# A constant tile made 288 bytes wider, in a hybrid decoder block on one core

## The chip, the cores and the metric

The kernel runs on one core of a Trainium2 chip. The metric is the device time of one launch in microseconds (us), the median over several runs. A profile is one execution of the program, recorded by the hardware profiler; its times are counted from the first instruction.

## What is computed

A sequence of 2048 rows of 1024 numbers, with 16 learned rows ahead of it, goes through one decoder layer in float32. Cut to what matters here:

```python
n1 = rmsnorm(h, norm1_g)
proj = n1 @ w_in                                  # 1024 -> 512 (S5 group) + 512 (pooling group)
ys = s5_mixer(proj[..., :512], ...)               # complex diagonal scan, GELU, GLU
yp = pool_mixer(proj[..., 512:], ...)             # trailing means over 2/4/8/16, linear map
h = h + concat([rmsnorm(ys), rmsnorm(yp)]) @ w_out
n2 = rmsnorm(h, norm2_g)
ff = silu(n2 @ w_gate) * (n2 @ w_up)              # 1024 -> 2816, twice
h = h + ff @ w_down                               # 2816 -> 1024
out = rmsnorm(h, final_norm_g)
```

The three large products of the last part (gate, up, down) are most of the arithmetic.

## The kernel before

**Products in three parts.** Every float32 operand of a large product is split into a high part (rounded to the type that TensorE multiplies, `fp32r`) and a low part (the rest). `split` writes the high part with ScalarE (L110) and the low part with VectorE (L85). `mm3` then makes three matmuls for one product of a 128x128 block with a 128x512 block:

```python
def mm3(o, lh, ll, rh, rl, first, last):          # L116
    PE.matmul(o, lh, rh, start=first, stop=False) # L117
    PE.matmul(o, lh, rl, start=False, stop=False) # L118
    PE.matmul(o, ll, rh, start=False, stop=last)  # L119
```

The second argument is the stationary operand (128x128, loaded into the array by a weight load ahead of the matmul), the third the moving operand (128x512, read through while the matmul runs). In the profile a matmul is written out<-moving,stationary: `pr<-xt3h,wch` reads `xt3h` as the moving operand.

**Stages.** (1) 0 to 300 us: input projection, parameters of the S5 group, scans; its large matmuls are `pj`, with the weights `wh`, `wl` moving. (2) 300 to 577 us: gates and output projection, large matmuls `po`, again with `wh`, `wl` moving. (3) 577 to 1450 us: the gate and up products, `pr`. (4) 1450 to 1884 us: the down product, `pd`, final norm and output.

**Stage 3.** `gate_up` runs for two halves of the sequence (`b`) and 11 pairs of column blocks (`f0`), and calls `seven` twice, for gate and for up: 44 calls. `seven` is one step of Strassen's scheme in its seven-product form: instead of eight products of 512-wide blocks it makes seven, each of 4 blocks x 3 matmuls = 12 matmuls, with additions before and after. The seven moving operands are tiles called `xb11`, `xb21`, `xt2`, `xt3`, `xt1`, `xt4`, `xb22`, in this order of use, each as a high and a low tile of 128 x 4 x 512 float32. The stationary operands `wch`, `wcl` are split from the loaded weights `raw` (and from their sums `s`) just ahead of use, into ten buffers each.

**Stage 4.** The same scheme over the down product: 7 products x 8 row blocks = 56 accumulations of 11 blocks x 3 matmuls. The moving operand is the split down weight, held in chunks of four blocks in four slots (`db11`, `db21`, `dt2`, `dt3`) that take turns; these slots are the stage 3 tiles of the same names without the d. The stationary operands `fh`, `fl` come from `fr`, loaded from memory.

**Where the tiles lie.** SBUF is handed out as two stacks in each partition: pools opened on the left grow upwards from the low addresses, pools opened with `side="right"` grow downwards from the top. The order of the pools' opening and the sizes of the tiles fix every address. In the program before these are, in bytes from the partition's start:

| side | tiles | begin at | modulo 512 |
|---|---|---|---|
| left | `ident`, `ones`, `mhalf` | 16512, 17024, 17056 | 128, 128, 160 |
| left | `xb11`, `xb21`, `xb22`, `xt1` (high and low; `db11`, `db21` in stage 4) | 22208 to 79552, 8192 apart | 192 |
| left | `raw`, `hr`, `xp`, `wr`, `dwr` (four shared buffers) | 87744 to 100032; end at 104128 | 192 |
| right | `xt2`, `xt3`, `xt4` (high and low; `dt2`, `dt3` in stage 4) | 104416 to 145376, 8192 apart | 480 |
| right | `wch`, `wcl` (`fh`, `fl`) | 188384 to 227296, 2048 apart | 480 |
| right | `wh`, `wl` (moving in stages 1 and 2) | 163808 to 221152 | 480 |
| right | `xh`, `xl`, `mh`, `ml` (stationary in stages 1 and 2) | 104672 to 133344 | 224 |

In stages 3 and 4, 288 bytes are free between the end of the left stack and the beginning of the right one.

**The touched tile.** `mhalf` holds the exponent -0.5. It is filled once (L127) and read by GpSimd's power instruction in `rsqrt_into` as `mhalf[:n, :m]`, with `m` of 1, 2 or 8. It is the third tile of the first left pool, so that all other large left tiles lie above it.

**What sets the order.** The kernel is written in the order of the loops; the build puts the instructions of each engine in order by its own estimate of times, and adds the semaphore waits. Nearly all transfers are issued from SyncE's queue.

Of the kernel before, what the change touches and what calls it, by code (L numbers as in the profile page):

```python
# [9 lines left out]
F32 = mybir.dt.float32  # L10
# [6 lines left out]
P = 128  # L17
# [7 lines left out]
T = 8  # L25
# [12 lines left out]
def kernel(  # L38
# [30 lines left out]
    const = ctx.enter_context(tc.tile_pool(name="const", bufs=1))  # L69
# [53 lines left out]
    make_identity(nc, ident)  # L123
    ones = const.tile([P, 1], F32, name="ones")
    V.memset(ones, 1.0)
    mhalf = const.tile([P, 2 * T], F32, name="mhalf")
    V.memset(mhalf, -0.5)  # L127
    ss2 = const.tile([P, 2, NB * T], F32, name="ss2")
    rs2 = const.tile([P, NB * T], F32, name="rs2")
# [1125 lines left out]
```

## Time and profile before

| what | value |
|---|---|
| runs | 1882.72, 1887.77, 1888.33 us; median 1887.77 |
| the profiled execution | 1885.98 us, span of its instructions 1884.2 us |
| granted TensorE clock, mean | 0.988 |
| TensorE matmuls | busy 97% of the span, 8497 instructions |
| VectorE, ScalarE, GpSimd | busy 65%, 36%, 43% |
| transfers | 298.37 MB, mean 158 GB/s |

A matmul's row names its line, its operands and its duration. Matmuls are pipelined: one of 0.39 us starts some 0.23 us after the one before. So the time that a stream of them takes is read from the starts in the timeline, not from the durations.

### The profile page before, as it was taken

What the parts mean: (1) busy time and instruction counts of PE and PEld (TensorE: products, weight loads), DVE (VectorE), ACT (ScalarE), POOL (GpSimd) and SP (SyncE); (2) the same over time, 40 slices, a digit from 0 to 9 for tenths busy, and PEclk for the clock granted to TensorE, in tenths of its full rate; (3) what the DMA queues carried; (4) which work ended last, traced back from release to release, by engine and by line L of the source; (5) the groups of instructions that cost most, each with busy time, mean ns of one, the idle gap of its engine ahead of it and who ended that gap; (6) DMA issues with size and microseconds to landing.
All of it is one profiled execution on the core that took longest, in us unless ns stands there. A gap on an engine that the chain in (4) does not pass through costs nothing.

```text
span 1884.2 us, 23676 instructions
## 1 busy us (share of the span) xinstructions
PE 1822.9 (97%) x8497; PEld 1495.4 (79%) x8497; DVE 1232.4 (65%) x1913; ACT 673.8 (36%) x1213; POOL 816.9 (43%) x619
## 2 busy tenths in 40 slices
PE   7989997899999999999999999999999999999998
PEld 5767786788887888888887788888888888888886
DVE  6996777866457866656667866766666444445763
ACT  4333334243454333332334332333223343333441
POOL 1684425633344565453656866665662000003400
PEclk9999998999999999999999999999999999999999
DMA  6255424444355344443436554554447765536771
GB/s 182 72 176 183 144 96 145 174 168 140 112 175 167 106 157 140 140 157 107 156 117 211 194 166 151 163 179 150 133 150 228 227 198 170 154 109 208 245 218 69
DMA packets 260518, 298.37 MB, mean 158 GB/s; under 512 B 17148, under 2 KB 204048, under 8 KB 255536
## 3 DMA queue, kind: packets, MB, share of 16 engines
q1 hardware_dynamic: 260304, 296.84, 49.5%
q8 instruction: 67, 1.10, 0.2%
q14 instruction: 51, 0.42, 0.1%
q0 software_dynamic: 96, 0.01, 0.0%
HBM read 202.37 MB, written 96.53 MB: 159 GB/s over the span
## 4 chain that ended last, share of the span: by engine, by line
PE 73%; DVE 3%; DMA 2%; POOL 1%; issue 1%; ACT 1%; DVEq 0%; POOLq 0%; ACTq 0%
PE pr L117 14%; PE pr L118 14%; PE pr L119 14%; PE pd L117 8%; PE pd L118 8%; PE pd L119 8%; PE po L117 2%; PE po L119 2%; PE po L118 2%; DVE wcl L85 1%; PE pgate L774 1%; DMA hr<-h_d 1%; PE ptx L865 1%; DMA xp<-xr_d 0%; PE ppool L760 0%
## 5 line engine op out<-in xcount | busy, mean ns | idle before, releaser
L110 ACT CAST wch<-raw 128x512 fp32r<-128x512 f32 x176 | 108.7, 621 | 268.2 <-PE pr L118 240.8
L85 DVE TENSOR_TENSOR wcl<-raw,wch 128x512 fp32r<-128x512 f32 x176 | 175.7, 1001 | 37.4 <-ACT wch L110 37.0
L85 DVE TENSOR_TENSOR fl<-fr,fh 128x512 fp32r<-128x512 f32 x168 | 116.9, 707 | 126.3 <-ACT fh L110 126.2
L110 ACT CAST fh<-fr 128x512 fp32r<-128x512 f32 x168 | 96.2, 584 | 202.4 <-PE pd L118 175.0
L110 ACT CAST wch<-s 128x512 fp32r<-128x512 f32 x132 | 82.1, 622 | 224.2 <-PE pr L118 174.6
L85 POOL TENSOR_TENSOR s<-raw 128x512 f32<-128x512 f32 x44 | 67.8, 1540 | 174.7 <-DVE wcl L85 75.3
L85 DVE TENSOR_TENSOR wcl<-s,wch 128x512 fp32r<-128x512 f32 x132 | 118.3, 896 | 19.4 <-ACT wch L110 19.1
L85 POOL TENSOR_TENSOR db22h<-db22h,hd 128x512 f32<-128x512 f32 x4 | 5.2, 1292 | 256.2 <-DVE db22h L85 256.2
L117 PE MATMUL pj<-wh,xh 128*128 128x512 f32 x256 | 102.6, 409 | 2.6 <-ACT xh L110 2.3
L117 PE MATMUL po<-wh,mh 128*128 128x512 f32 x256 | 103.8, 406 | 0.7 <-ACT mh L110 0.7
L119 PE MATMUL pj<-wh,xl 128*128 128x512 f32 x256 | 103.0, 407 | 0.0
L118 PE MATMUL pj<-wl,xh 128*128 128x512 f32 x256 | 102.7, 403 | 0.0
L119 PE MATMUL po<-wh,ml 128*128 128x512 f32 x256 | 100.4, 393 | 0.8 <-DVE ml L85 0.8
L118 PE MATMUL po<-wl,mh 128*128 128x512 f32 x256 | 100.7, 393 | 0.0
L85 POOL TENSOR_TENSOR rs<-rv,mhalf 128x1 f32<-128x1 f32 (+2 forms) x35 | 31.5, 900 | 154.1 <-DVE rv L91 144.8
L85 POOL TENSOR_TENSOR wr<-wr 128x512 f32<-128x512 f32 x44 | 66.8, 1519 | 72.4 <-DMA wr<-in_w_down_dram 64.5
L85 DVE TENSOR_TENSOR gt<-gt,ut 128x512 f32<-128x512 f32 x88 | 92.9, 1057 | 0.0
L85 POOL TENSOR_TENSOR tmp<-z,pk 64x512 f32<-64x512 f32 x32 | 50.8, 1588 | 79.8 <-issue 64.7
L85 DVE TENSOR_TENSOR gt<-pr,gt 128x512 f32<-128x512 f32 x66 | 45.5, 690 | 60.3 <-PE pr L119 60.1
L85 POOL TENSOR_TENSOR ut<-gt 128x512 f32<-128x512 f32 x22 | 33.6, 1528 | 107.2 <-DVE gt L85 107.2
L117 PE MATMUL pr<-xt2h,wch 128*128 128x512 f32 x176 | 70.5, 400 | 5.3 <-DVE gt L85 3.6
L1006 ACT ACTIVATE gt<-gt 128x512 f32<-128x512 f32 x88 | 55.6, 633 | 50.8 <-DVE gt L85 50.8
(392 smaller groups left out, 5586.1 us busy)
## 6 DMA issues: line engine op xcount, KB each, us to landing
fr<-ff_d SPq DMA_DIRECT2D x56, 704.0 KB, 4.9
raw<-in_w_gate_dram SPq DMA_DIRECT2D x44, 512.0 KB, 4.8
raw<-in_w_up_dram SPq DMA_DIRECT2D x44, 512.0 KB, 4.3
ff_d<-gt SPq DMA_DIRECT2D x22, 1024.0 KB, 3.9
pk<-pk_d SPq DMA_DIRECT2D x16, 1284.0 KB, 6.2
ff_d<-ut SPq DMA_DIRECT2D x22, 768.0 KB, 5.6
wr<-in_w_down_dram SPq DMA_DIRECT2D x22, 512.0 KB, 3.3
wd_d<-wr SPq DMA_DIRECT2D x22, 512.0 KB, 3.4
```

Of the source, the lines that this page charges most:

```text
L85: e.tensor_tensor(o, a, b, op=op)
L110: A.copy(hi, src)
L117: PE.matmul(o, lh, rh, start=first, stop=False)
L118: PE.matmul(o, lh, rl, start=False, stop=False)
L119: PE.matmul(o, ll, rh, start=False, stop=last)
L774: PE.matmul(pg[:, k * P:(k + 1) * P], glubd[:, k], gt[:, k], start=True, stop=True)
L865: PE.transpose(pt[:, k], r[:, (4 * h + k) * P:(4 * h + k + 1) * P], ident)
L1006: lambda i, j: A.activation(gt[:, i, j], gt[:, i, j], AF.Silu), b == 0 and f0 == 0)
```

## The change

`mhalf` is allocated with 72 more words (288 bytes) in each partition, and its fill covers them too; no instruction reads the new words.

```diff
-    mhalf = const.tile([P, 2 * T], F32, name="mhalf")
+    mhalf = const.tile([P, 2 * T + 72], F32, name="mhalf")
     V.memset(mhalf, -0.5)
```

All left tiles after `mhalf` move up by 288 bytes: those at 192 modulo 512 come to lie at 480. The left stack of stages 3 and 4 now ends at 104416, where the right one begins. Right tiles stay where they are. The moving operand and the stationary operand of every large matmul then begin at the same address modulo 512 in stages 3 and 4, whichever side the moving one lies on.

## The prediction

> **What bounds the kernel now.** I read the page first: the share of each engine, then the chain of work that ended last.
>
> ```profile
> span 1884.2 us, 23676 instructions
> ...
> PE 1822.9 (97%) x8497; PEld 1495.4 (79%) x8497; DVE 1232.4 (65%) x1913; ACT 673.8 (36%) x1213; POOL 816.9 (43%) x619
> ...
> PE 73%; DVE 3%; DMA 2%; POOL 1%; issue 1%; ACT 1%; DVEq 0%; POOLq 0%; ACTq 0%
> PE pr L117 14%; PE pr L118 14%; PE pr L119 14%; PE pd L117 8%; PE pd L118 8%; PE pd L119 8%; PE po L117 2%; PE po L119 2%; PE po L118 2%; DVE wcl L85 1%; PE pgate L774 1%; DMA hr<-h_d 1%; PE ptx L865 1%; DMA xp<-xr_d 0%; PE ppool L760 0%
> ```
>
> TensorE carries 73% of the chain, and 66% of it are the matmuls of stages 3 and 4 (`pr` 3 x 14, `pd` 3 x 8). Next the busy time by stretch, and who waits for whom.
>
> ```profile
> core 0: us, PE busy (x) PEld busy (x) DVE busy (x) ACT busy (x) POOL busy (x), PEclk, DMA share, GB/s
> ...
> 575.00:1000.00 425.00, 422.42 (x1849) 342.22 (x1848) 291.32 (x370) 152.93 (x260) 224.29 (x150) 1.00 0.44 139
> 1000.00:1050.00 50.00, 45.94 (x192) 36.37 (x191) 39.69 (x45) 24.24 (x43) 38.66 (x26) 0.97 0.63 210
> 1050.00:1445.00 395.00, 395.00 (x1709) 321.00 (x1708) 271.51 (x330) 128.33 (x208) 243.52 (x160) 1.00 0.51 164
> 1450.00:1816.00 366.00, 366.00 (x1587) 297.69 (x1586) 185.64 (x266) 134.97 (x238) 44.57 (x35) 1.00 0.63 191
> ```
>
> ```profile
> ACT wch L110 <- PE pr L118: 415.4, 226, 2.2
> ...
> ACT fh L110 <- PE pd L118: 175.0, 109, 2.2
> ```
>
> From 1050 to 1816 us TensorE has no idle time at all, at the full granted clock. The longest waits are those of ScalarE for matmuls to give `wch` and `fh` buffers back: the producers run ahead and wait for TensorE. So a matmul that takes less time shortens these stages one for one, until VectorE (291.32 of 425 us, 69%) or GpSimd (243.52 of 395 us, 62%) would be full.
>
> **What the left tiles have to do with it.** The change moves addresses, so I compared matmuls that differ in the moving operand alone. Rows of the answers by tile; the three numbers are the shortest, median and longest duration in ns.
>
> ```profile
> L117 PE MATMUL pr<-xt1h,wch x176: 395/396/397, 583.9 to 1444.3; 128*128 128x512 f32 x176
> L117 PE MATMUL pr<-xb22h,wch x176: 392/396/397, 586.7 to 1449.9; 128*128 128x512 f32 x176
> L117 PE MATMUL pr<-xt3h,wch x176: 389/389/503, 592.0 to 1441.5; 128*128 128x512 f32 x176
> L117 PE MATMUL pd<-db11h,fh x176: 392/396/397, 1450.6 to 1876.0; 128*128 128x512 f32 x176
> L117 PE MATMUL pd<-db21h,fh x144: 395/396/397, 1453.4 to 1815.6; 128*128 128x512 f32 x144
> L117 PE MATMUL pd<-dt3h,fh x152: 389/389/395, 1511.9 to 1873.9; 128*128 128x512 f32 x152
> L117 PE MATMUL po<-wh,mh x256: 387/389/500, 303.2 to 576.4; 128*128 128x512 f32 x128
> ```
>
> Every matmul with its moving operand on the left (192 modulo 512: `xt1`, `xb22`, `db11`, `db21`) has a median of 396, every one with it on the right (480: `xt3`, `dt3`, `wh`) 389. The shapes are equal, and so is the stationary tile within each stage. The spread inside a group is smaller than the step. The durations are modelled, so the price is read from starts: the first matmul of each of the seven products of one call of `seven`, and the first of the next call.
>
> ```profile
> 701.25 0.40 PE L117 MATMUL pr<-xb11h,wch 128*128 128x512 f32 x1
> ...
> 704.05 0.40 PE L117 MATMUL pr<-xb21h,wch 128*128 128x512 f32 x1
> ...
> 706.85 0.39 PE L117 MATMUL pr<-xt2h,wch 128*128 128x512 f32 x1
> ...
> 709.60 0.39 PE L117 MATMUL pr<-xt3h,wch 128*128 128x512 f32 x1
> ...
> 712.32 0.40 PE L117 MATMUL pr<-xt1h,wch 128*128 128x512 f32 x1
> ...
> 715.12 0.39 PE L117 MATMUL pr<-xt4h,wch 128*128 128x512 f32 x1
> ...
> 717.87 0.40 PE L117 MATMUL pr<-xb22h,wch 128*128 128x512 f32 x1
> ...
> 720.67 0.40 PE L117 MATMUL pr<-xb11h,wch 128*128 128x512 f32 x1
> ```
>
> Twelve matmuls from the left take 2.80 us (`xb11`, `xb21`, `xt1`, `xb22`), from the right 2.72 us (`xt3`), and 2.75 us for `xt2` and `xt4`, the two that follow a left product. That is 233.3 against 226.7 ns a matmul. The same in stage 4:
>
> ```profile
> 1570.79 0.40 PE L117 MATMUL pd<-db21h,fh 128*128 128x512 f32 x1
> ...
> 1572.89 0.40 PE L117 MATMUL pd<-dt2h,fh 128*128 128x512 f32 x1
> ...
> 1575.62 0.39 PE L117 MATMUL pd<-dt3h,fh 128*128 128x512 f32 x1
> ...
> 1578.34 0.40 PE L117 MATMUL pd<-db11h,fh 128*128 128x512 f32 x1
> ```
>
> Nine from the left in 2.10 us (233.3 ns), twelve of `dt3` in 2.72 us (226.7 ns).
>
> **The change part by part.**
> The first part is the wider fill, 88 words instead of 16.
>
> ```profile
> 0.85 0.07 DVE L127 MEMSET mhalf<- 128x16 f32 x1
> ...
> 1.07 0.09 DVE L498 MEMSET eb<- 128x32 f32 x1
> 3.85 0.17 DVE L289 COPY vcol<-vp 128x8 f32<-128x8 f32 x1 [2.69 <-PE vp L288]
> ```
>
> 16 more words cost 0.02 us by the fills before and after, so 72 more about 0.1 us. VectorE is idle for 2.69 us behind the fills; they hide it. Without that cover it would be 0.1 us. I count 0. If the build's order changed with the longer fill, that would be another program; the idle time behind the fill makes it unlikely.
>
> The second part is the moving operand of stages 3 and 4 at 480 instead of 192. No row shows a left tile at 480. The nearest rows bound it: 389 ns as every right tile (gain), 396 as now (nothing), and below nothing one more step of the same size. I take 389: after the change, moving and stationary operands begin exactly as those of `xt3` and `wch` do, and not only modulo 512, since 104416 minus 22496 (`xt2h` and the new `xb11h`) is 5 x 16384. Of what could tell the two kinds apart, only the distance along the partition is left.
>
> The sum. One call of `seven` takes 720.67 - 701.25 = 19.42 us; with seven products of 2.72 us it takes 19.04, so 0.38 less. There are 44 calls (176 matmuls of a kind, four a call): 16.7 us. Stage 4 has 3 x 176 `db11` and 3 x 144 `db21` matmuls: 960 x 6.7 ns = 6.4 us. `dt2` after a left chunk takes 2.73 us, so nothing is added there. Together 23.1 us.
>
> What of it is off the path: at the beginning of stage 3 and between its two halves the chain runs through others, as these pieces of it show.
>
> ```profile
> 1005.61 4.03 DMA xp<-xr_d
> ...
> 1020.11 3.40 DVE xt4l L85 x2
> ...
> 1030.75 5.80 DMA wr<-in_w_down_dram
> ```
>
> About three calls of the 44 lie in such stretches, and there a shorter matmul only makes a longer wait: 3 x 0.38 = 1.1 us. Left over are 22 us. Stages 1 and 2 move `wh` from the right and gain nothing. The profiled execution took 1885.98 us, 1.8 us under the median of 1887.77; from it the sum gives 1864, from the median 1866. I forecast 1865 us.
>
> The third part is the transfers to and from left tiles, which also begin at 480 instead of 192.
>
> ```profile
> fr<-ff_d SPq DMA_DIRECT2D x56, 704.0 KB, 4.9
> raw<-in_w_gate_dram SPq DMA_DIRECT2D x44, 512.0 KB, 4.8
> raw<-in_w_up_dram SPq DMA_DIRECT2D x44, 512.0 KB, 4.3
> ```
>
> `raw` lands at 192 and `fr` at 480, both in runs of 128 words; 512 KB take 4.3 to 4.8 us, 704 KB 4.9. Per KB the one at 480 is the faster. I count nothing, between a gain of 1 and a loss of 2 us (a twentieth of the 2% of the chain that are transfers). [...] No row here separates the two offsets for reads out of SBUF.
>
> **The rivals.**
> First, nothing happens, because the step belongs to the place and not to the offset. All moving tiles with 389 ns lie at or above 104416 and all with 396 below 87744, so the trace of before cannot exclude it. Against it: inside each side the rows do not drift with the address (`db11h` at 22208 and `xt1h` at 71360 both 396), while `dt3` and `wh` lie 43 KB and more apart and both have 389. A step without any slope looks like an offset. Time: 1886 us, within the runs of before.
> [...]
>
> Second, slower. The left tiles begin at multiples of 64 now (192) and will not (480). If straddling 64-byte blocks cost a matmul in the low addresses one more step of 6.7 ns, the 3072 left matmuls (12 x 176 + 960) would lose 20.5 us: 1906. Against it: the right tiles straddle the same way and have 389 ns. It would decide as soon as the median of a left matmul were above 396.
>
> Third, half the gain: the matmuls become faster, but the producers stop being ahead, with VectorE or GpSimd the bound in stage 3. For it speaks only GpSimd's and VectorE's share of 62 and 69%; against it, that the stage gets 2% shorter while 31% of VectorE is free, and that ScalarE's waits for buffers (415.4 us) are long. Time: about 1876.
>
> **How the numbers follow.** The whole gain 0.80, half of it 0.04, nothing 0.13, slower 0.03. The first has a range of its own of 1858 to 1872 (the sum and the spread of the runs). The range of 8 in 10 takes in the half gain: 1857 to 1879. It leaves out the rival "nothing" and the slower one, 0.16 together. Differences under 0.3%, 5.7 us, are what a measurement of this kernel cannot tell from no change; the runs of before are that far apart. Faster by more than that 0.84, within 0.13, slower 0.03.
>
> **What would show it.** In the profile after, the medians of `xt1h`, `xb22h`, `db11h` and `db21h` stand at 389, one call of `seven` takes 19.04 us, `xt2` and `xt4` come down to 2.72 us, and `xt3` stays. The stretch of stage 3 gets some 16 us shorter, that of stage 4 some 6, stages 1 and 2 stay. ScalarE's waits for `pr` become shorter by about as much. The prediction is wrong if the left medians stay at 396 (place, not offset), or if they fall and new waits of TensorE for `wch` or `xp` appear.

## The result, and the profile after

With the change the kernel takes 1867.8 us (median of six runs, 1867.15 to 1872.35), before 1888.69 us (six runs, 1882.72 to 1890.76). The ratio is 0.9897, 95% interval 0.9881 to 0.9913: about 20 us, or 1%, less. The forecast was 1865 us in a range of 1857 to 1879. The profiled execution took 1867.75 us, its instructions a span of 1866.0.

The page after: its span, the busy time, and the first rows of the chain.

```profile
span 1866.0 us, 23676 instructions
...
PE 1803.0 (97%) x8497; PEld 1498.3 (80%) x8497; DVE 1240.0 (66%) x1913; ACT 672.6 (36%) x1213; POOL 815.2 (44%) x619
...
PE 71%; DVE 3%; DMA 2%; POOL 1%; issue 1%; ACT 1%; POOLq 0%; DVEq 0%; SPq 0%; ACTq 0%
```

The instructions are the same in number and, on every engine, in order; one of them, the fill of `mhalf`, is longer. TensorE's busy time is 19.9 us less, and it is still the bound. By tile, after (shortest, median and longest duration in ns):

```profile
L117 PE MATMUL pr<-xb11h,wch x176: 388/390/499, 581.4 to 1422.5; 128*128 128x512 f32 x176
L117 PE MATMUL pr<-xt1h,wch x176: 388/390/390, 587.3 to 1433.4; 128*128 128x512 f32 x176
L117 PE MATMUL pr<-xb22h,wch x176: 388/390/502, 590.0 to 1438.9; 128*128 128x512 f32 x176
L117 PE MATMUL pr<-xt3h,wch x176: 388/390/506, 595.5 to 1430.7; 128*128 128x512 f32 x176
L117 PE MATMUL pd<-db11h,fh x176: 388/390/390, 1439.5 to 1857.7; 128*128 128x512 f32 x176
L117 PE MATMUL pd<-dt3h,fh x152: 388/390/390, 1499.4 to 1855.7; 128*128 128x512 f32 x152
```

The left tiles have come down from 396 to 390, and no side differs from the other any more. One call of `seven` in the timeline, first matmuls of its products:

```profile
703.11 0.39 PE L117 MATMUL pr<-xb11h,wch 128*128 128x512 f32 x1
...
705.83 0.39 PE L117 MATMUL pr<-xb21h,wch 128*128 128x512 f32 x1
...
708.55 0.39 PE L117 MATMUL pr<-xt2h,wch 128*128 128x512 f32 x1
...
711.27 0.39 PE L117 MATMUL pr<-xt3h,wch 128*128 128x512 f32 x1
```

Each product takes 2.72 us, `xt2` behind a left product too.

The first matmul of stage 3 stood at 577.9 us before:

```profile
L117 PE MATMUL pr<-xb11h,wch x176: 392/396/501, 577.9 to 1433.2; 128*128 128x512 f32 x176
```

With the first matmuls of stage 4 (1450.6 before, 1439.5 after), stage 3 went from 872.7 to 858.1 us (14.6 less), and stage 4 up to the end of the span from 433.6 to 426.5 (7.1 less). Stages 1 and 2 took 3.5 us more. The operands of their large matmuls lie where they lay; what differs is the granted clock, which in this execution fell in the midst of stage 2. The window of 543 to 552 us, first before, then after; the column after POOL is the clock.

```profile
543.00:552.00 9.00, 8.12 (x49) 7.16 (x50) 4.37 (x9) 3.60 (x10) 5.78 (x5) 1.00 0.29 109
```

```profile
543.00:552.00 9.00, 7.42 (x24) 6.30 (x25) 4.39 (x9) 3.74 (x9) 5.77 (x5) 0.62 0.37 118
```

At 0.62 of the clock TensorE started 24 instead of 49 matmuls. The two experiments below with the same gain have a clock of 1.00 in this window and begin stage 3 at 575.3 and 575.7 us; the run with the left tiles at 416, which gains nothing, has 0.62 too, and its first `xt1h` matmul comes at 588.1 us (583.9 before, 587.3 after). Without the fall the spans would differ by about 22 us, an estimate from the 18.2 us between them and these 3.5.

### The profile page after: what moved, and what is told of

Same layout as the page of the kernel before. It is cut to its first block, busy times and chain, and to the rows that moved or that the text cites. A ratio compares the mean times of both kernels' runs of the same rounds, so it can differ in the third digit from the quotient of the medians.

```text
span 1866.0 us, 23676 instructions
## 1 busy us (share of the span) xinstructions
PE 1803.0 (97%) x8497; PEld 1498.3 (80%) x8497; DVE 1240.0 (66%) x1913; ACT 672.6 (36%) x1213; POOL 815.2 (44%) x619
## 4 chain that ended last, share of the span: by engine, by line
PE 71%; DVE 3%; DMA 2%; POOL 1%; issue 1%; ACT 1%; POOLq 0%; DVEq 0%; SPq 0%; ACTq 0%
PE pr L117 13%; PE pr L119 13%; PE pr L118 13%; PE pd L118 7%; PE pd L117 7%; PE pd L119 7%; PE po L117 2%; PE po L119 2%; PE po L118 2%; DVE wcl L85 1%; POOL s L85 1%; PE pgate L774 1%; DMA hr<-h_d 1%; PE ptx L865 1%; DMA raw<-in_w_gate_dram 1%
## 5 line engine op out<-in xcount | busy, mean ns | idle before, releaser
L117 PE MATMUL pj<-wh,xh 128*128 128x512 f32 x256 | 103.3, 411 | 2.3 <-ACT xh L110 2.3
L117 PE MATMUL po<-wh,mh 128*128 128x512 f32 x256 | 104.6, 409 | 0.7 <-ACT mh L110 0.7
L117 PE MATMUL pr<-xt2h,wch 128*128 128x512 f32 x176 | 69.7, 396 | 6.1 <-DVE gt L85 3.6
```

## The experiments

Since the change worked, the question was what a good address is. Two things were open: whether the moving tile's own address counts (ABS) or its distance to the stationary tile (REL), and by which modulus (M64 stands for 64, and so on). "Before" in each comparison is the kernel before, run on the same chip.

### Four offsets in one kernel

```diff
-    mhalf = const.tile([P, 2 * T], F32, name="mhalf")
+    mhalf = const.tile([P, 2 * T + 8], F32, name="mhalf")
...  # xb11l, xb21l, xb22l allocated 8 words longer, the rest of the row unused
```

> The four left pairs lie at four offsets modulo 512: xb11 at 224, xb21 at 256, xb22 at 288, xt1 at 320; stationary tiles stay at 480. Theory M64 (what counts is the remainder modulo 64, 32 is good and 0 is not): xb11 and xb22 at 389 ns, xb21 and xt1 at 396; one call of seven takes about 19.04 + 2 x 0.08 + 0.03 = 19.2 us. Theory M512 (the remainder modulo 512 must be that of the stationary tile): all four stay at 396, a call takes 19.4 us. Theory M128 (96 modulo 128 as in 480 and 224): xb11 389, the three others 396.

It took 1881.55 us (one run; before 1882.69, seven runs). Its timeline:

```profile
702.74 0.40 PE L117 MATMUL pr<-xb21h,wch 128*128 128x512 f32 x1
...
705.54 0.40 PE L117 MATMUL pr<-xt2h,wch 128*128 128x512 f32 x1
...
711.02 0.40 PE L117 MATMUL pr<-xt1h,wch 128*128 128x512 f32 x1
...
713.83 0.40 PE L117 MATMUL pr<-xt4h,wch 128*128 128x512 f32 x1
...
716.59 0.40 PE L117 MATMUL pr<-xb22h,wch 128*128 128x512 f32 x1
...
719.35 0.40 PE L117 MATMUL pr<-xb11h,wch 128*128 128x512 f32 x1
```

`xb21` at 256 takes 2.80 us and `xt1` at 320 takes 2.81, as bad as before. `xb22` at 288 takes 2.76. `xb11` at 224, behind `xb22`, takes 2.77 (median of its products in the trace). The rows do not fit any of the three expectations alone, and one of them shows why: `xt4`, which nobody moved, takes 2.76 us behind `xt1`, as it took 2.75 before. A product that is off leaves its mark on the product behind it. So offsets cannot be mixed in one kernel to be read cleanly; in stage 4, where `db11` stands behind other neighbours, the offset 224 reads 389 ns.

### Both sides at 192

```diff
+    rpad = ctx.enter_context(tc.tile_pool(name="rpad", bufs=1, side="right")).tile([P, 72], F32, name="rpad")
+    V.memset(rpad, 0.0)
     mid = ExitStack()
```

> The whole right stack is moved down by 288 bytes, the left one stays as before: all moving and stationary tiles of stages 3 and 4 begin at 192 modulo 512, in stages 1 and 2 the moving wh, wl at 192 and the stationary tiles at 448. Theory REL (only the distance between moving and stationary tile counts): all medians 389, time 1866 to 1869 as with the change. Theory ABS (the moving tile's own address counts): every moving tile is now at a bad offset, all medians 396; 2472 more matmuls of stages 3 and 4 and about 1500 of stages 1 and 2 lose 6.7 ns, 17 to 25 us: 1904 to 1914.

1863.24 us, ratio 0.9887 (0.9854 to 0.9920): the gain of the change, with the left tiles where they always were. By tile:

```profile
L117 PE MATMUL pr<-xt1h,wch x176: 389/389/389, 581.2 to 1427.3; 128*128 128x512 f32 x176
...
L117 PE MATMUL pr<-xt3h,wch x176: 389/389/495, 589.4 to 1424.5; 128*128 128x512 f32 x176
...
L117 PE MATMUL po<-wh,mh x256: 387/389/500, 300.7 to 573.7; 128*128 128x512 f32 x128
```

192 is no bad address. ABS falls, REL stands. In stage 2 the moving `wh` lies at 192 and the stationary `mh` at 448 here, 256 apart, and nothing is lost.

### The stationary tiles at nine offsets

```diff
-        hi = wc_p.tile([P, 4, P], F32R, name="wch", tag="wch", bufs=10)
+        hi = hi_tile("wch")   # nine tiles wcha to wchi in turn, each 32 bytes longer
```

The same for `fh`, and a fill of 56 words that keeps the right moving tiles at 480.

> As before (left moving tiles at 192, right ones at 480), but the high stationary tiles take nine buffers a to i at 192, 224, 256, ... 448 modulo 512 in turn, and the low ones lie at 224. Theory ABS: the letter makes no difference, left 396, right 389 for each. Theory REL modulo 64: with a, c, e, g, i (multiples of 64) the left tiles come down to about 389 and the right ones go up to about 396; with b, d, f, h as before. Theory REL modulo 512: left is good with a only.

1891.9 us (one run). `xt3h` lies at 480 as ever; the letter is the stationary buffer (`a` at 192, `b` at 224, `i` at 448).

```profile
L117 PE MATMUL pr<-xt3h,wchb x20: 387/389/389, 609.8 to 1326.8; 128*128 128x512 f32 x20
L117 PE MATMUL pr<-xt3h,wchi x20: 390/397/397, 630.6 to 1346.3; 128*128 128x512 f32 x20
...
L117 PE MATMUL pr<-xt3h,wcha x20: 397/397/475, 710.3 to 1424.3; 128*128 128x512 f32 x20
L117 PE MATMUL pr<-xt3h,wchh x20: 392/393/394, 729.8 to 1443.8; 128*128 128x512 f32 x20
L117 PE MATMUL pr<-xt3h,wchd x16: 394/394/396, 770.5 to 1307.4; 128*128 128x512 f32 x16
```

The same moving tile has 389 with the buffer that lies 256 bytes from it modulo 512, and 392 to 397 with the other eight. By the starts the picture is less sharp, since the stationary buffer changes with every product and the marks carry over: with `b` the seventh to eleventh matmuls come 226 to 227 ns apart, but all twelve take 2.75 us, no less than with `h`; with the other seven buffers it is 2.77 to 2.81 (medians in the trace). So this run speaks for REL, but does not show alone that 0 modulo 256 is best. The expected pattern modulo 64 did not come: the right tiles with `d` or `h`, odd multiples of 32 like 480, were to stay at 389 and did not. The left tiles' rows are mixed in the same way and were of no use, by the carrying over seen above.

### Eight words instead of 72

```diff
-    mhalf = const.tile([P, 2 * T], F32, name="mhalf")
+    mhalf = const.tile([P, 2 * T + 8], F32, name="mhalf")
```

> mhalf is 8 words wider instead of 72: all large left tiles at 224 modulo 512, right ones at 480. Theory M64 or M128 or M256: the whole gain, 1866 to 1869 us, left medians 389. Theory M512: no change, 1883 to 1890, left medians 396.

1864.27 us, ratio 0.9896 (0.9863 to 0.9930): the whole gain with 32 bytes.

```profile
L117 PE MATMUL pr<-xb22h,wch x176: 389/389/402, 584.4 to 1433.6; 128*128 128x512 f32 x176
L117 PE MATMUL pr<-xt1h,wch x176: 389/389/389, 581.7 to 1428.1; 128*128 128x512 f32 x176
```

Left tiles at 224 are as good as at 480. The modulus is not 512.

### The sides change places

```diff
+    rpad = ...tile([P, 72], F32, name="rpad")          # as above: the right stack down to 192
-    wch, fh: bufs=10
+    wch, fh: bufs=9
+    fill = ...tile([P, 56], F32, name="fill")          # xt2, xt3, xt4 back to 480
```

> Left moving tiles at 192 as before, all stationary tiles of stages 3 and 4 moved to 192, right moving tiles kept at 480 (nine buffers of wch instead of ten make the room). No moving tile changes its offset against the kernel before. Theory REL: the two sides change places, left medians 389, right medians (xt2, xt3, xt4, dt2, dt3) 396; 3072 matmuls gain and 2472 lose 6.7 ns, about 1881 against 1885. Theory ABS (after the run with both sides at 192 already unlikely): left 396, right 389, no change.

```profile
L117 PE MATMUL pd<-db21h,fh x144: 389/389/402, 1453.9 to 1816.1; 128*128 128x512 f32 x144
L117 PE MATMUL pd<-dt2h,fh x144: 391/397/399, 1457.1 to 1874.2; 128*128 128x512 f32 x144
```

In the timeline:

```profile
700.70 0.40 PE L117 MATMUL pr<-xb22h,wch 128*128 128x512 f32 x1
...
703.46 0.39 PE L117 MATMUL pr<-xb11h,wch 128*128 128x512 f32 x1
...
706.18 0.39 PE L117 MATMUL pr<-xb21h,wch 128*128 128x512 f32 x1
...
711.70 0.39 PE L117 MATMUL pr<-xt3h,wch 128*128 128x512 f32 x1
...
714.50 0.40 PE L117 MATMUL pr<-xt1h,wch 128*128 128x512 f32 x1
...
720.06 0.40 PE L117 MATMUL pr<-xb22h,wch 128*128 128x512 f32 x1
```

They did change places: `xb11` takes 2.72 us now and `xt3` 2.80, and neither has changed its offset modulo 512. The time was expected 4 us under before and is 0.14% over it (1889.66 against 1886.96, ratio 1.0014, interval 1.0001 to 1.0026). Part of the miss is the carrying over, which I had left out: `xb22` behind a bad product takes 2.76 us, so a call takes 19.36 us, against 19.42 before, and all 44 gain 2.6 us. In the profiled execution stage 3 is indeed 2.7 us shorter (870.0 against 872.7), but stage 4 is 2.5 longer (436.1 against 433.6), where `db11` takes 230.0 ns a matmul from start to start and not 226.7, and stages 1 and 2 are 3.3 longer (581.2 against 577.9). The rest was not tried apart; the nine buffers instead of ten, and with them another order of instructions on several engines, also differ.

### Three more distances

Only the number of added words differs from the eight above: 24, 40 and 56.

> mhalf 24 words wider: left tiles at 288, 64 modulo 128 away from the stationary tiles at 480. If the distance counts modulo 64: all medians 389 and about 1866. If modulo 128 or 256: left above 389, 1875 to 1887.

> mhalf 40 words wider: left tiles at 352, 128 modulo 256 away from the stationary tiles. If the distance counts modulo 64 or 128: all medians 389 and about 1866. If modulo 256: left above 389, 1875 to 1887.

> mhalf 56 words wider: left tiles at 416, 64 below the stationary tiles at 480 (192 modulo 256). Modulo 64: all medians 389, about 1866. Modulo 128 or 256: left above 389; if the sign of the distance does not matter, as in the run with the left tiles at 288.

They took 1882.76, 1885.08 and 1889.14 us (one run each; before 1886.96, 1881.99 to 1890.28): no gain that these single runs can tell. The timelines, in the same order:

```profile
704.39 0.39 PE L117 MATMUL pr<-xb11h,wch 128*128 128x512 f32 x1
...
707.14 0.39 PE L117 MATMUL pr<-xb21h,wch 128*128 128x512 f32 x1
```

```profile
701.32 0.40 PE L117 MATMUL pr<-xb11h,wch 128*128 128x512 f32 x1
...
704.12 0.40 PE L117 MATMUL pr<-xb21h,wch 128*128 128x512 f32 x1
```

```profile
705.00 0.39 PE L117 MATMUL pr<-xb11h,wch 128*128 128x512 f32 x1
...
707.80 0.39 PE L117 MATMUL pr<-xb21h,wch 128*128 128x512 f32 x1
```

2.75, 2.80 and 2.80 us. So the modulus is neither 64 (all three would be good) nor 128 (352 would be). All kernels in which one distance rules a product:

| moving minus stationary, modulo 256 | where seen | twelve matmuls, us | ns each |
|---|---|---|---|
| 0 | the change; 224 against 480; 192 against 192 | 2.72 | 226.7 |
| 32 | right tiles, sides changed (480 against 192) | 2.80 | 233.3 |
| 64 | left tiles at 288 | 2.75 | 229.2 |
| 128 | left tiles at 352 | 2.80 | 233.3 |
| 192 | left tiles at 416 | 2.80 | 233.3 |
| 224 | before (192 against 480) | 2.80 | 233.3 |

96 was seen only among mixed neighbours, 160 only with the stationary tiles in turn. The run with four offsets fits the table afterwards: `xb21` lay at distance 32 (2.80 us), `xb22` at 64 (2.76), `xb11` at 0 behind a product that was off. No tried distance is better than 0, so no version beats the change; the one with 8 words has the same gain for 32 bytes.

## Why the prediction was right, point by point

**The bound.** TensorE is the bound of stages 3 and 4, and they got shorter by nearly all that the matmuls lost. ScalarE's waits for buffers fell, and that for `wch` remains the longest:

```profile
ACT wch L110 <- PE pr L118: 390.4, 220, 3.1
...
ACT fh L110 <- PE pd L118: 165.0, 103, 2.2
```

**The size.** 0.38 us a call was foretold and measured: four left products of 2.80 and two of 2.75 became 2.72. Expected were 16 us in stage 3 and 6 in stage 4, measured 14.6 and 7.1. The sum of 22 us came out in the two stages as 21.7, so closely in part by luck, as two of its terms missed in opposite directions. Of the 16.7 us of the 44 calls 2.1 did not arrive, where 1.1 had been put for the pieces off the path; the run with eight words, where stage 3 is 14.2 us shorter, says the same. And `dt2` behind a left chunk had been put at nothing, from one product of 2.73 us. By all its starts it took 228.2 ns a matmul before and 226.7 after; over 432 matmuls that is 0.6 us more gain in stage 4. The forecast of 1865 is 2.8 us under the median. The 3.5 us of stages 1 and 2, where the clock fell, show how much one execution can differ by; what the 2.8 us are is not shown.

**Readings that were too broad.** Not every tile on the right had 389: `xt2h`, behind a left product, had a median of 392 (L117) before, and single matmuls of a group took up to 503 ns. The wait for `fh` was the third longest; GpSimd waited longer for `db22h`, 256.2 us. The sum used neither reading.

**The fill.** Foretold was 0.1 us more behind idle time; it took 0.13 instead of 0.07 us, and the copy behind it started at 3.83 instead of 3.85 us.

```profile
0.86 0.13 DVE L127 MEMSET mhalf<- 128x88 f32 x1
...
3.83 0.17 DVE L289 COPY vcol<-vp 128x8 f32<-128x8 f32 x1 [2.61 <-PE vp L288]
```

**The transfers.** `raw` now lands at 480:

```profile
raw<-in_w_gate_dram SPq DMA_DIRECT2D x44, 512.0 KB, 4.8
raw<-in_w_up_dram SPq DMA_DIRECT2D x44, 512.0 KB, 4.6
```

4.8 and 4.6 us after 4.8 and 4.3: the run with both sides at 192, where `raw` did not move, has 4.8 and 4.7, so the offset does not show. No run shows the twentieth from which the prediction had its loss of 2 us; of the transfers out of left tiles `xr_d<-hr` took 4.2 us before and after, `wd_d<-wr` 3.4 and 3.5.

**The rivals.** Place instead of offset fell with the change itself; the run with the sides changed shows the places with their prices exchanged. By this rival the time would have stayed; it fell by 1%, with 288 bytes and with 32. The slower rival (blocks of 64 bytes) fell: 480 is no multiple of 64 and good. The half gain fell too: from 1050 to 1445 us TensorE was busy for 394.29 of 395 us after the change, VectorE for 286.72.

**What the prediction did not say.** It spoke of the offset of the moving tile, "480 instead of 192", and took 389 because everything about the new address would equal that of `xt3`. The number did not depend on whose offset counts. The runs showed that it is the distance to the stationary tile modulo 256. The row of `po` (moving 480, stationary 224) in the prediction already held half of that: 256 apart and good.

How the two operands lie to each other changes the time from matmul to matmul by up to 6.7 ns in 226.7. The rows of the weight loads themselves stay (`xb11h`: median 188 ns before and after). Why the distance counts is not shown, and a matmul without its weight load was not tried.

## What to carry to other kernels

Group equal matmuls by their operands before looking for the cause of a long stage: a step of 2 to 3% that is larger than the usual spread inside the groups, on the engine that is the bound, is worth finding. Here it goes away when moving and stationary tiles begin at the same address modulo 256, which costs a few words of padding in a tile that is allocated early. Compare starts, not durations, and do not mix offsets in one run.

## What the runs showed that I had not expected

The distance 64 modulo 256 costs 2.5 ns a matmul, and 32, 128, 192 and 224 cost 6.7 each: the price is not a ramp, and 64 bytes above the stationary tile's remainder are cheaper than 64 below it (192). And the price is carried over: in the kernel before, `xt2` and `xt4` need 2.75 us behind a left product although their own distance is good, and with the sides changed `xb22` needs 2.76 behind a right one. In the timeline before, the carrying over ends within one product, since `xt3` behind `xt2` is at 2.72; by the starts it is the first five matmuls of the twelve that are slower. What it is that needs these matmuls to fall back into step stays open.
